# A ring of weight halves moved to six different distances (modulo 512 bytes) from the operands it is multiplied with

## The chip, the core and the metric

One NeuronCore of a Trainium2 chip runs the whole program. The metric is the device time of one execution in microseconds (us); the kernel before has a median of 2301.32 us over three runs. About 0.2% (4.6 us) is what a measurement of this kernel can tell from no change.

## The reference

One layer of a transformer-like trunk on a sequence of 512 tokens of width 2048, all in float32. With modulation vectors from a small matrix-vector product (`mod = silu(c) @ w_ada + b_ada`), it computes

```
h    = rms_norm(x) * (1 + sc1) + sh1
proj = h @ w_in                        # 2048 -> 7168 columns, seven groups of 1024
o_hg = gated linear recurrence (8 heads) on four of the groups
o_sb = stick-breaking attention (8 heads) on three of the groups
x    = x + g1 * (concat(o_hg, o_sb) @ w_out)      # 2048 -> 2048
h    = rms_norm(x) * (1 + sc2) + sh2
x    = x + g2 * ((silu(h @ w_gate) * (h @ w_up)) @ w_ffn_out)   # 2048 -> 2 x 5632 -> 2048
```

## The kernel before

**Three products for one.** Nearly all matrix products run in the format `float32r`. To keep float32's precision each operand is split in two halves: `hi`, the value rounded to `float32r`, and `lo`, the rest. One 128x128 block of a product is then three matmuls, `whi*xhi`, `whi*xlo` and `wlo*xhi`, added up in PSUM: in every group of three, two matmuls use a hi half of the weights and one a lo half. The halves of the weights are made on the fly by `split` (lines 212-222): ScalarE copies the raw tile into `hi` (line 220), VectorE subtracts `hi` from the raw tile into `lo` (line 221).

**The ring.** The halves live in the pool `wp`, in tiles of 4096 bytes per partition: tag `hi` with three buffers and tag `lo` with three buffers, six tiles in all, used in turn. The raw weights come into four tiles of 8192 bytes of the same pool. In the FFN, and after it, every fourth split goes to a spare pair instead (`spare[0]`, line 215): in the gate/up products that is a pair of tiles `hi2`, `lo2` in the pool `tp` (line 1106), whose matmuls the profile calls `ff_1hi`, `ff_1lo` and so on, where those of the ring are `ff_1h`, `ff_1l`; in the last product the pair lies inside an operand buffer (`spare_there`, line 1165).

**Where the tiles lie in a partition.** Pools are laid out one behind the other from the low end (constants, `wp`, the operands `hhi` and `hlo`, then `opA`, `opD` and others), and a few (`xop`, `tp`, `rp`, `zp`) from the high end downward. In `wp` the four raw tiles come first, then the three hi tiles at bytes 43808, 47904 and 52000, then the three lo tiles at 56096, 60192 and 64288. `hhi` starts at 68384, `hlo` at 101152, `opA` at 133920, `opD` at 166688. All these differ by multiples of 512 bytes. The spare pair `hi2`, `lo2` lies at 215008 and 219104: 146624 = 286 x 512 + 192 bytes above `hhi`, so its distance modulo 512 is 192. One column of a block is 4 bytes in each partition, a 128-column block of weights 512 bytes; every slice that a matmul of the ring takes starts a whole number of 512 bytes into its tile.

**Stages, in the order of the program**, and which operand of the matmul the ring's half is (a matmul loads its *stationary* operand of 128 columns with a weight load, and streams its *moving* operand past it):

- `st` (lines 286-332): hgrn2's values, 512 columns of ring half moving past slices of `hhi`/`hlo`.
- `sbp` (`sb_project`, line 337): attention's projections, 384 columns of ring half moving, with the attention itself (matmuls in plain float32) woven in.
- `hgf`, `hgq`, `hgg` (`mtile`, line 599): ring half stationary, 512 columns of `hhi`/`hlo` moving, with the recurrence woven in.
- `wo` (`wo_part`, line 808): ring half stationary, 512 columns moving; then its last tile and the first FFN columns (lines 917-980) with 256 columns moving.
- `ffA`, `ffB`, `ffC` (lines 1115-1157): the gate and up products in Strassen's form. For each of 42 column blocks there are seven products of 24 matmuls (8 blocks of the width times three), ring half or spare half stationary, 256 columns of `opA` to `opD` moving.
- `foA`, `foB`, `foC` (`multiply`, line 1183): the last product, also in Strassen's form, ring half moving with 512 columns.

The order of TensorE's work is written out by the program, with a small planner (`Clock`) that weaves in the attention and recurrence by estimated times. The tile framework adds the waits: a new tile of a ring position waits until the matmuls that read the old one are through.

Of the kernel before, what the change touches and what calls it, by code (L numbers as in the profile page):

```python
# [11 lines left out]
F32R = mybir.dt.float32r  # L12
# [5 lines left out]
P = 128  # L18
# [111 lines left out]
def trunk(ctx, tc, a):  # L130
# [6 lines left out]
    wp = ctx.enter_context(tc.tile_pool(name="wp", bufs=3))  # L137
# [6 lines left out]
    def acc(name):  # L144
        return psum.tile([P, T], F32, tag="acc", name=name)
# [22 lines left out]
    def small_col(base, i=0):  # L168
        return small[:, base + i:base + i + 1]
# [9 lines left out]
    def gemv(w, row, col):  # L179
        V.scalar_tensor_tensor(w, w, 1.0, row, op0=ALU.mult, op1=ALU.mult, accum_out=col)  # L180

    def finish_gain(comp, k0, k1):
        g, base = (gain1, C_N1) if comp == SC1 else (gain2, C_N2)
        V.scalar_tensor_tensor(g[:, k0:k1], mod[:, comp * KT + k0:comp * KT + k1], 1.0, small[:, base + k0:base + k1],
                               op0=ALU.add, op1=ALU.mult)

    def ada(comp, k):
        j = comp * KT + k
        c = slice(j, j + 1)
        gemv(row_load(a["w_ada"][j], f"ada{j}"), cond, mod[:, c])  # L190
        left[comp] -= 1
        if comp == SC1:
            V.tensor_add(mod[:, c], mod[:, c], small_col(C_BADA, j))
            finish_gain(comp, k, k + 1)
        elif not left[comp]:
            all_k = slice(comp * KT, comp * KT + KT)
            V.tensor_add(mod[:, all_k], mod[:, all_k], small[:, C_BADA + comp * KT:C_BADA + comp * KT + KT])
            if comp == SC2:
                finish_gain(comp, 0, KT)
# [7 lines left out]
        nc.sync.dma_start(r, src)  # L207
        return r

    spare, count = [], [0]  # L210

    def split(r, shape, name):
        count[0] += 1
        if spare and count[0] % 4 == 0:
            hi, lo = spare[0](shape, name)
        else:
            hi = wp.tile(shape, F32R, tag="hi", name=name + "h")
            lo = wp.tile(shape, F32R, tag="lo", name=name + "l")
        with tc.high_priority(offset=AHEAD):
            S.copy(hi, r)  # L220
            V.tensor_sub(lo, r, hi.bitcast(F32))  # L221
        return hi, lo

    def weights(src, shape, name):
        return split(load(src, shape, name), shape, name)
# [60 lines left out]
    for k in range(KT):  # L286
        xk = xo[:, k]
        if k == 0:
            for i in range(2):
                sl = slice(i * 1024, i * 1024 + 1024)  # L290
                gemv(r0[:, sl], cond[:, sl], lead[:, i:i + 1])
            j = SC1 * KT
            V.scalar_tensor_tensor(mod[:, j:j + 1], lead[:, 0:1], lead[:, 1:2], small_col(C_BADA, j), op0=ALU.add, op1=ALU.add)
            finish_gain(SC1, 0, 1)
            whi = wp.tile([P, 1024], F32R, tag="hi", name="wi0h")
            wlo = wp.tile([P, 1024], F32R, tag="lo", name="wi0l")
            for sl in (slice(0, T), slice(T, 2 * T)):
                S.copy(whi[:, sl], w0[:, sl])
                V.tensor_sub(wlo[:, sl], w0[:, sl], whi[:, sl].bitcast(F32))
        else:  # L300
            nc.sync.dma_start(xk, a["x"][:, k])
            ada(SC1, k)
            if k == 2:
                nc.sync.dma_start(cst, a["cst"])
            if k == KT - 1:
                nc.sync.dma_start(ident2, a["cst"][:, 0])
            whi, wlo = weights(a["w_hi"][k], [P, 1024], f"wi{k}")
        gk = gain1[:, k:k + 1]
        S.activation(hhi[:, k], xk, AF.Identity, scale=gk)
        V.scalar_tensor_tensor(hlo[:, k], xk, gk, hhi[:, k].bitcast(F32), op0=ALU.mult, op1=ALU.subtract)  # L310
        if k == 0:
            S.activation(ss1, xk, AF.Square)
        else:
            sq = sb.tile([P, T], F32, tag="qT" if k % 2 else "kT", name=f"sq{k}", bufs=1)
            S.activation(sq, xk, AF.Square)
            V.tensor_add(ss1, ss1, sq)
        for n in range(2):
            for t in range(4):
                ts_ = slice(t * P, t * P + P)
                cs = slice(n * T, n * T + T)  # L320
                out = banks[n * 4 + t]
                PE.matmul(out, hhi[:, k, ts_], whi[:, cs], start=(k == 0), stop=False)
                PE.matmul(out, hhi[:, k, ts_], wlo[:, cs], start=False, stop=False)
                PE.matmul(out, hlo[:, k, ts_], whi[:, cs], start=False, stop=(k == KT - 1))
# [12 lines left out]
    def sb_project(h):  # L337
        ps = [acc(f"sbp{h}_{t}") for t in range(4)]
        for c in range(8):
            if c % 2 == 0:  # L340
                raw = load(a["w_sb"][h, c // 2], [P, 2, 2, 384], f"wsb{h}_{c}")
            whi, wlo = split(raw[:, c % 2], [P, 2, 384], f"wsb{h}_{c}")
            pairs = [(kk, t) for kk in range(2) for t in range(4)]
            if c in (0, 7):
                pairs.sort(key=lambda p: p[1])
            for kk, t in pairs:
                k = 2 * c + kk
                ts_ = slice(t * P, t * P + P)
                out = ps[t][:, 0:384]
                PE.matmul(out, hhi[:, k, ts_], whi[:, kk], start=(k == 0), stop=False)  # L350
                PE.matmul(out, hhi[:, k, ts_], wlo[:, kk], start=False, stop=False)
                PE.matmul(out, hlo[:, k, ts_], whi[:, kk], start=False, stop=(k == KT - 1))
                clock.run()
        clock.until(lambda: h not in reuse or reuse[h] in done)
        if h in (0, 3):
            rows = scr[:, 0:3].rearrange("p a b -> p (a b)").rearrange("p (t c) -> p t c", t=4)
        else:
            rows = sb.tile([P, 4, 384], F32, tag="rows", name=f"rows{h}")
        for t in range(4):
            if t % 2:  # L360
                V.tensor_copy(rows[:, t], ps[t][:, 0:384])
            else:
                S.copy(rows[:, t], ps[t][:, 0:384])
        ready[h] = rows
# [234 lines left out]
    def mtile(src, name, xhi, xlo, out, nk=KT):  # L599
        n = 0  # L600
        raw = load(src, [P, nk, P], name)
        for c0 in range(0, nk, HALF):
            w = min(HALF, nk - c0)
            whi, wlo = split(raw[:, c0:c0 + w], [P, w, P], f"{name}_{c0}")
            for kk in range(w):
                three(out, whi[:, kk], wlo[:, kk], xhi[:, c0 + kk], xlo[:, c0 + kk], n == 0, n == nk - 1)
                n += 1
                clock.run()
# [314 lines left out]
    for i, hs in enumerate(halves):  # L923
        out = acc(f"wo{m}h{i}")[:, 0:HT]
        n = 0
# [304 lines left out]
    for u, (c, i) in enumerate(units):  # L1230
# [15 lines left out]
        for q, p in enumerate(ORDER):  # L1246
            out = {2: B[i], 7: C, 4: C}.get(p, A)
# [104 lines left out]
```

## Time and profile before

| | |
|---|---|
| three runs | 2303.38, 2301.32, 2300.13 us; median 2301.32 us |
| profiled execution, first to last instruction | 2299.2 us |
| TensorE (PE) busy | 2249.4 us, 98% of the span, 14171 matmuls |
| VectorE (DVE) busy | 1917.8 us, 83% |
| ScalarE (ACT) busy | 1160.6 us, 50% |
| DMA engines | 53% of the span, 190 GB/s on average |
| mean granted TensorE clock | 0.994 |

The profile gives the span of the profiled execution and not a device time of its own beside it; the span lies 2.1 us under the median of the runs. A row of a view of the profile names the line, the engine, the operation and the tiles (`out<-in,in`: for a matmul the moving operand first, then the stationary one), how many there were, the busy time and the mean duration of one in ns. Matmuls are pipelined, so the duration of one (about 280 ns) is longer than the time from the start of one to the start of the next, which is what a stream of matmuls costs; that pace is read from start times in the view in order of time.

### The profile page before, as it was taken

The numbers are of one execution on the slowest core, as the hardware profiler recorded it, in microseconds if no ns is written. First come the engines' busy times: TensorE is split into PE (matmuls) and PEld (weight loads), VectorE is DVE, ScalarE is ACT, GpSimd is POOL, SyncE is SP. The second block draws the span as 40 slices with busy tenths as digits, with TensorE's granted clock in tenths as the row PEclk, the third lists the DMA queues.
The fourth block names the chain that finished last, engine by engine and source line by source line (L and its number), as shares of the span: only waits on it lengthen the run. The fifth ranks groups of instructions, "written<-read, shape, count | busy, mean of one in ns | idle before, by whom it ended". The sixth has DMA issues, their size and how long they took to land.

```text
span 2299.2 us, 35729 instructions
## 1 busy us (share of the span) xinstructions
PE 2249.4 (98%) x14171; PEld 2050.2 (89%) x14171; DVE 1917.8 (83%) x2566; ACT 1160.6 (50%) x2015; POOL 10.7 (0%) x25
## 2 busy tenths in 40 slices
PE   7999899999999999999999999999999999999999
PEld 6899899888888788999999999999999977778787
DVE  8887779999888865699899988888888778888888
ACT  4316666565655522564454445454545544544453
POOL 0000000000000000000000000000000000000000
PEclk9999999999999999999999999999999999999999
DMA  9885546853322386346555645454443486665452
GB/s 368 319 317 218 174 145 227 304 183 111 128 93 74 130 303 214 105 151 225 189 204 185 220 143 175 143 174 143 150 160 129 166 314 232 238 220 213 154 200 76
DMA packets 114978, 437.69 MB, mean 190 GB/s; under 512 B 9822, under 2 KB 58236, under 8 KB 76796
## 3 DMA queue, kind: packets, MB, share of 16 engines
q1 hardware_dynamic: 114812, 435.42, 53.0%
q8 instruction: 111, 1.82, 0.3%
q14 instruction: 55, 0.45, 0.1%
HBM read 386.61 MB, written 48.77 MB: 189 GB/s over the span
## 4 chain that ended last, share of the span: by engine, by line
PE 77%; DVE 13%; DMA 3%; issue 3%; ACT 3%; SPq 0%; DVEq 0%; ACTq 0%
PE ffA L93 18%; PE foA L93 9%; PE ffC L93 9%; PE sbp L93 7%; PE wo L93 7%; PE foC L93 4%; PE ffB L93 4%; PE st L93 4%; PE hgf L93 4%; PE hgq L93 3%; PE hgg L93 3%; DMA opd<-fhi 1%; DVE ada L180 1%; DVE yraw L1190 1%; PE l L93 1%
## 5 line engine op out<-in xcount | busy, mean ns | idle before, releaser
L180 DVE SCALAR_TENSOR_TENSOR ada<-ada,cond 128x2048 f32<-128x2048 f32 x95 | 216.8, 2286 | 54.5 <-DMA ada<-in_w_ada 54.3
L93 PE MATMUL ffA<-opD,ff_3h 128*128 128x256 f32 x512 | 93.9, 284 | 1.8 <-ACT u L1018 1.7
L93 PE MATMUL ffA<-opB,ff_6h 128*128 128x256 f32 x512 | 94.1, 284 | 1.0 <-ACT ff_6h L220 1.0
L93 PE MATMUL ffB<-opA,ff_2h 128*128 128x256 f32 x512 | 93.5, 283 | 0.0
L93 PE MATMUL ffC<-opC,ff_4h 128*128 128x256 f32 x512 | 93.5, 283 | 0.0
L93 PE MATMUL ffA<-opC,ff_5h 128*128 128x256 f32 x496 | 90.7, 283 | 0.8 <-ACT b L1018 0.8
L93 PE MATMUL ffA<-opA,ff_1h 128*128 128x256 f32 x496 | 90.6, 283 | 0.0
L93 PE MATMUL ffC<-opB,ff_7h 128*128 128x256 f32 x496 | 90.6, 283 | 0.0
L221 DVE TENSOR_TENSOR wfo_0l<-wfo,wfo_0h 128x1024 fp32r<-128x1024 f32 x48 | 58.7, 1224 | 37.9 <-ACT wfo_0h L220 37.5
L93 PEld LDWEIGHTS ffA<-opD,ff_3h 128*128 128x128 f32 x512 | 79.7, 192 | 2.4 <-ACT u L1018 2.4
L93 PEld LDWEIGHTS ffA<-opB,ff_6h 128*128 128x128 f32 x512 | 80.1, 193 | 1.3 <-ACT ff_6h L220 1.2
L93 PEld LDWEIGHTS ffC<-opC,ff_4h 128*128 128x128 f32 x512 | 79.7, 192 | 0.0
L93 PEld LDWEIGHTS ffB<-opA,ff_2h 128*128 128x128 f32 x512 | 79.7, 192 | 0.0
L220 ACT CAST wfo_0h<-wfo 128x1024 fp32r<-128x1024 f32 x48 | 50.6, 1054 | 57.5 <-PE foA L93 50.4
L1092 ACT CAST fhi<-forms 128x512 fp32r<-128x512 f32 (+1 forms) x63 | 43.6, 692 | 68.5 <-DMA opd<-fhi 59.2
L93 PEld LDWEIGHTS ffA<-opC,ff_5h 128*128 128x128 f32 x496 | 77.2, 192 | 1.0 <-ACT b L1018 1.0
L93 PEld LDWEIGHTS ffC<-opB,ff_7h 128*128 128x128 f32 x496 | 77.3, 192 | 0.0
L93 PEld LDWEIGHTS ffA<-opA,ff_1h 128*128 128x128 f32 x496 | 77.2, 192 | 0.0
L93 PE MATMUL ffA<-opB,ff_6l 128*128 128x256 f32 x256 | 72.7, 284 | 0.0
L93 PE MATMUL ffC<-opC,ff_4l 128*128 128x256 f32 x256 | 72.4, 283 | 0.0
L93 PE MATMUL ffA<-opD,ff_3l 128*128 128x256 f32 x256 | 72.4, 283 | 0.0
L93 PE MATMUL ffB<-opA,ff_2l 128*128 128x256 f32 x256 | 72.4, 283 | 0.0
(1646 smaller groups left out, 7764.6 us busy)
## 6 DMA issues: line engine op xcount, KB each, us to landing
ada<-in_w_ada SPq DMA_DIRECT2D x95, 1024.0 KB, 5.2
wfo<-in_w_fo SPq DMA_DIRECT2D x16, 1024.0 KB, 5.9
yraw<-in_w_fo SPq DMA_DIRECT2D x16, 1024.0 KB, 4.8
fix<-in_w_fix SPq DMA_DIRECT2D x14, 1024.0 KB, 5.6
opd<-forms SPq DMA_DIRECT2D x44, 256.0 KB, 4.3
opd<-fhi SPq DMA_DIRECT2D x42, 256.0 KB, 4.3
opsC<-opd SPq DMA_DIRECT2D x10, 1024.0 KB, 5.1
opsA<-opd SPq DMA_DIRECT2D x9, 1024.0 KB, 7.2
```

What stands on the lines that cost most here:

```text
L93: self.engine.matmul(out, lhsT, rhs, **kw)
L180: V.scalar_tensor_tensor(w, w, 1.0, row, op0=ALU.mult, op1=ALU.mult, accum_out=col)
L220: S.copy(hi, r)
L221: V.tensor_sub(lo, r, hi.bitcast(F32))
L1092: S.copy(hi, R[:, q])
L1190: V.tensor_sub(*(t[:, k0:k0 + w] for t in (d, e, g)))
```

## The change

The tags `hi` and `lo` with three buffers each are replaced by six tags with one buffer each, used as three pairs in turn. Each tile is longer than its 4096 bytes of content by 64 to 384 bytes, and the content begins at an offset inside it. The spare pairs, the number and the order of all instructions on each engine's data, and all shapes stay.

```diff
+    pads = ((("h0", 64, 0), ("l0", 64, 0)), (("h1", 256, 0), ("l1", 128, 0)), (("h2", 192, 0), ("l2", 224, 32)))
+
+    def ring_pair(shape, name):
+        n = int(np.prod(shape[1:]))
+        out = []
+        for tag, before, after in pads[turns[0] % 3]:
+            t = wp.tile([P, 1024 + (before + after) // 4], F32R, tag=tag, name=name + tag[0], bufs=1)
+            t = t[:, before // 4:before // 4 + n]
...
+            out.append(t)
+        turns[0] += 1
+        return out
 
     def split(r, shape, name):
...
         else:
-            hi = wp.tile(shape, F32R, tag="hi", name=name + "h")
-            lo = wp.tile(shape, F32R, tag="lo", name=name + "l")
+            hi, lo = ring_pair(shape, name)
...
-            whi = wp.tile([P, 1024], F32R, tag="hi", name="wi0h")
-            wlo = wp.tile([P, 1024], F32R, tag="lo", name="wi0l")
+            whi, wlo = ring_pair([P, 1024], "wi0")
```

The six tiles take 4160, 4160, 4352, 4224, 4288 and 4352 bytes, 25536 together instead of 24576. Counted from the first, their contents begin at 64, 4224, 8576, 12800, 17088 and 21408. Everything laid out behind `wp` from the low end moves up by 960 bytes, `hhi` to 25536 behind the ring's start; what is laid out from the high end stays. Each content's start less `hhi`'s start, modulo 512, is then

| tile | h0 | l0 | h1 | l1 | h2 | l2 | spare pair of the FFN |
|---|---|---|---|---|---|---|---|
| distance before | 0 | 0 | 0 | 0 | 0 | 0 | 192 |
| distance after | 128 | 192 | 448 | 64 | 256 | 480 | 256 |

For example h0: 64 - 25536 = -25472, and -25472 + 50 x 512 = 128. The spare pair comes to 192 - 960 + 1024 = 256. `hlo` and `opA` to `opD` lie multiples of 512 behind `hhi`, so the row holds for them too. Where the ring's half is the moving operand, the distance of the stationary operand from it is the same number with its sign turned (128 becomes 384, 480 becomes 32).

More of the change, by code (lines that the diff above doesn't have):

```diff
@@ L208, in load @@
         return r
-    spare, count = [], [0]
+    spare, count, turns = [], [0], [0]
+    pads = ((("h0", 64, 0), ("l0", 64, 0)), (("h1", 256, 0), ("l1", 128, 0)), (("h2", 192, 0), ("l2", 224, 32)))
[5 more added lines that the diff above has]
+            t = t[:, before // 4:before // 4 + n]
+            if len(shape) == 3:
+                t = t.rearrange("p (a b) -> p a b", a=shape[1])
+            elif len(shape) == 4:
+                t = t.rearrange("p (a b c) -> p a b c", a=shape[1], b=shape[2])
+            out.append(t)
+        turns[0] += 1
+        return out
     def split(r, shape, name):
```

## The prediction

> **What bounds the kernel now.** I read first the page's busy times and the shares of the chain that ended last.
>
> ```profile
> PE 2249.4 (98%) x14171; PEld 2050.2 (89%) x14171; DVE 1917.8 (83%) x2566; ACT 1160.6 (50%) x2015; POOL 10.7 (0%) x25
> PE 77%; DVE 13%; DMA 3%; issue 3%; ACT 3%; SPq 0%; DVEq 0%; ACTq 0%
> ```
>
> TensorE is busy in 98% of the span, and 77% of the chain is its own work. A busy TensorE need not be at its best pace, so the pace is the question. Next, busy times by stage, in the order st, sbp (two rows), hgf to hgg, wo, first FFN columns, ffA to ffC, foA to foC; the pairs behind the length are PE, PEld, DVE, ACT (POOL too), then clock, DMA share and GB/s.
>
> ```profile
> 0.00:101.00 101.00, 89.22 (x386) 73.55 (x387) 84.50 (x127) 44.80 (x60) 1.68 (x9) 1.00 0.94 353
> 101.00:235.00 134.00, 130.49 (x733) 128.17 (x732) 108.59 (x134) 51.99 (x91) 0.00 (x0) 0.97 0.73 268
> 235.00:439.00 204.00, 196.67 (x1163) 184.98 (x1161) 166.21 (x240) 126.14 (x340) 0.00 (x0) 0.97 0.55 197
> 439.00:770.00 331.00, 328.22 (x1678) 275.76 (x1677) 289.25 (x541) 201.53 (x444) 9.05 (x16) 1.00 0.36 131
> 770.00:943.00 173.00, 170.28 (x764) 139.29 (x763) 107.96 (x133) 52.63 (x82) 0.00 (x0) 1.00 0.62 220
> 943.00:1004.00 61.00, 60.61 (x492) 59.51 (x490) 55.49 (x142) 51.80 (x120) 0.00 (x0) 1.00 0.30 100
> 1004.00:1849.00 845.00, 838.33 (x7052) 836.89 (x7052) 726.56 (x822) 419.79 (x612) 0.00 (x0) 1.00 0.50 175
> 1849.00:2299.20 450.20, 435.61 (x1917) 352.05 (x1916) 379.23 (x433) 211.91 (x269) 0.00 (x0) 0.99 0.56 201
> ```
>
> TensorE is full in every stage but the first, where the DMA engines are at 94%. The gate/up stage alone is 845 us. Of the other engines VectorE comes next everywhere, between 62% and 91%.
>
> **The pace, ring against spare pair.** In order of time, a stretch of products with the ring's halves (the first column is the start in us; rows that hold two matmuls end in x2):
>
> ```profile
> 1209.98 0.40 PE L93 MATMUL ffA<-opD,ff_3h 128*128 128x256 f32 x2
> 1210.22 0.28 PE L93 MATMUL ffA<-opD,ff_3l 128*128 128x256 f32 x1
> 1210.34 0.40 PE L93 MATMUL ffA<-opD,ff_3h 128*128 128x256 f32 x2
> 1210.58 0.28 PE L93 MATMUL ffA<-opD,ff_3l 128*128 128x256 f32 x1
> 1210.70 0.40 PE L93 MATMUL ffA<-opD,ff_3h 128*128 128x256 f32 x2
> ```
>
> and one with the spare pair's:
>
> ```profile
> 1031.17 0.39 PE L93 MATMUL ffA<-opA,ff_1hi 128*128 128x256 f32 x2
> 1031.40 0.28 PE L93 MATMUL ffA<-opA,ff_1lo 128*128 128x256 f32 x1
> 1031.51 0.39 PE L93 MATMUL ffA<-opA,ff_1hi 128*128 128x256 f32 x2
> 1031.74 0.28 PE L93 MATMUL ffA<-opA,ff_1lo 128*128 128x256 f32 x1
> 1031.85 0.39 PE L93 MATMUL ffA<-opA,ff_1hi 128*128 128x256 f32 x2
> ```
>
> Three matmuls take 0.36 us with the ring (120.0 ns each) and 0.34 us with the spare pair (113.3 ns): the same instruction, shape and moving operands, 6.7 ns less. That this is no accident of one stretch shows in the groups of the gate/up stage, whose last number before the second bar is the mean ns of one:
>
> ```profile
> L93 PE MATMUL ffA<-opA,ff_1h 128*128 128x256 f32 x495 | 90.5, 283 | 0.0
> L93 PE MATMUL ffA<-opA,ff_1hi 128*128 128x256 f32 x176 | 30.5, 276 | 0.0
> ```
>
> Again 7 ns apart. By the layout, the ring's weights lie 0 from the operand modulo 512, the spare pair's 192. Now the other widths, 384 columns in order of time, then 512 columns from the chain (start, length, what, count):
>
> ```profile
> 149.97 0.33 PE L93 MATMUL sbp<-wsb_2h,hhi 128*128 128x384 f32 x1
> ...
> 150.49 0.33 PE L93 MATMUL sbp<-wsb_2h,hhi 128*128 128x384 f32 x1
> ```
>
> ```profile
> 11.78 87.71 PE st L93 x378
> 812.72 130.55 PE wo L93 x574
> 2001.37 8.18 PE foA L93 x36
> ```
>
> Three matmuls of 384 columns take 0.52 us, 173.3 ns each; 130.55/574 is 227.4 ns and 8.18/36 is 227.2 ns for 512 columns. From 256 to 384 to 512 columns each step of 128 costs 53 to 54 ns, 0.42 ns a column, so 256 columns alone are 106.7 ns. The ring pays about 13.3 ns per matmul on top, whatever the width and whether its half is stationary (wo) or moving (sbp, foA); the spare pair pays 6.7. A charge per matmul and not per column fits the weight load, which is the same 128 columns each time and runs beside the matmul. My theory: the load and the moving stream disturb each other when their addresses agree modulo 512 bytes, and each such meeting costs 6.7 ns, the time of 16 columns or 64 bytes.
>
> The Trainium skill says the opposite: in "TensorE: Matmul & The Clock Gate", Part 2, on LDWEIGHTS, TensorE has two independent read ports into the state buffer, so that loading the next weights takes no read bandwidth from the running matmul. By that the six distances change nothing; the 7 ns between the two groups above speak against it, unless the spare pair is quicker for another reason.
>
> **The change part by part.**
>
> *Instructions and waits.* None is added or removed. The positions are still used in turn, three deep, so each split waits for the same earlier product as now; cost nothing. These waits sit on ScalarE and are covered by the other two pairs:
>
> ```profile
> ACT ff_2h L220 <- PE ffA L93: 39.1, 26, 1.9
> PE st L93 <- ACT hhi L309: 11.8, 1, 11.8
> PE foA L93 <- ACT O L1205: 3.6, 1, 3.6
> ```
>
> The copies wait up to 1.9 us for their slot, while TensorE itself waits long only at the start.
>
> *ScalarE and VectorE.* The copy and the subtraction now read and write at unlike distances. The spare pair does so already (raw 192 away):
>
> ```profile
> L220 ACT CAST ff_1hi<-wg3r 128x1024 fp32r<-128x1024 f32 x1 | 1.1, 1060 | 0.0
> L220 ACT CAST ff_1h<-wg4r 128x1024 fp32r<-128x1024 f32 x1 | 1.1, 1057 | 1.3 <-issue 1.3
> L221 DVE TENSOR_TENSOR ff_1lo<-wg19r,ff_1hi 128x1024 fp32r<-128x1024 f32 x1 | 1.2, 1227 | 0.3 <-ACT ff_1hi L220 0.3
> L221 DVE TENSOR_TENSOR ff_1l<-wg20r,ff_1h 128x1024 fp32r<-128x1024 f32 x1 | 1.2, 1227 | 1.6 <-ACT ff_1h L220 1.6
> ```
>
> 1060 against 1057 and 1227 against 1227 ns: cost nothing. They also price the waits above if their cover were gone: a product would then start later by at most one split, 1.06 + 1.23 us.
>
> *The ring's matmuls.* No row shows 64, 128, 256, 448 or 480; the ends are the rows at 0 (13.3 ns on top) and at 192 (6.7 ns). I take 192's price for h0, l0, h1, l1 and h2, which lie 64 bytes or more from 0, and 0's price for l2, which lies 32 bytes from it (480 = 512 - 32), inside the 64 bytes of one meeting. Of three matmuls one uses a lo half, and of three lo halves one is l2: 8/9 of the ring's matmuls save 6.7 ns, 5.9 ns on average. Where TensorE has slack or VectorE is close, part is lost:
> - Gate/up: 42 x 7 products of 24, less 73 that go to the spare pair, leaves 5304 matmuls, 31.4 us. At these paces 5304 x 120.0 + 1752 x 113.3 ns is 835 of the stage's 845 us, so TensorE is the limit; VectorE would rise from 726.56/845 (86%) to 89%. I keep 30.
> - First FFN columns (384, and 96 of wo's last tile): 480 x 5.9 = 2.8; VectorE 91%, ScalarE 85%: half, 1.5.
> - sbp (8 heads x 16 x 4 x 3): 1536 x 5.9 = 9.1, in a stage woven with attention's chains: two thirds, 6.
> - hgf to hgg (24 tiles x 16 x 3): 1152 x 5.9 = 6.8; VectorE 87%: two thirds, 4.5.
> - wo (15 x 16 x 3): 720 x 5.9 = 4.3; DMA 62%: 3.5.
> - foA to foC: 3/4 of 1848 (22 x 2 x 7 x 2 x 3) matmuls are the ring's, 1386 x 5.9 = 8.2; VectorE 84%: two thirds, 5.5. Its spare pair lies inside an operand buffer and stays at 0.
> - st (16 x 8 x 3): 384 x 5.9 = 2.3 us; the DMA engines at 94% would be late next: nothing.
>
> *The spare pair of the gate/up stage* moves from 192 to 256. It could gain or lose up to 6.7 ns in each of 1752 matmuls, 11.7 us either way. I take nothing: 256 is nearer to 192 than to 0.
>
> Sum: 30 + 1.5 + 6 + 4.5 + 3.5 + 5.5 = 51 us. The profiled span of 2299.2 becomes 2248; the median of the runs, 2.1 us above it, becomes **2250 us**, 2.2% less.
>
> The same page of the Trainium skill, Part 1 ("Wait — 56ns, not 53.3ns?"), gives a warm matmul N/2.4 GHz plus about 2.5 ns, so an estimate by it is 109.2 ns for 256 columns; no row here shows a float32r matmul that fast.
>
> **The rivals.** If all six tiles paid 192's price, the sum would be 51 x 9/8 = 57 us (2244 us), the measure for what follows.
> 1. *Only tiles nearer to 192 than to 0 gain* (h0, l0, h2: 16 + 8 + 16 of every 72 matmuls, 5/9). For it: nothing is known between the rows. Against: the price comes in steps of 64 bytes. 57 x 5/9 = 32 us, 2269 us.
> 2. *The distance counts modulo 128 or 256.* Then 256 is as bad as 0 for h2 and the spare pair (modulo 128 also h0). Gain 5/9 of 57, less 11.7: 20 us, 2281 us; modulo 256 only h2 is lost among the hi halves (6/9 with l2 lost): 38 less 11.7, 2275 us. Against it only that I know of one good distance.
> 3. *Some distances are better than 192.* If half of the 6.7 ns that are left goes as well, the ring gains 57 x 1.5 = 86 and the spare pair 1752 x 3.3 = 5.8 us: 2209 us. For it: 6.7 ns still stand above the columns.
> 4. *The distance does nothing*, and the spare pair is quick for where it lies (the high end) or for its single buffer: 2301 us. For it: pace and place change together in the only two cases known. The rule of the Trainium skill quoted above is of this kind.
> 5. *Slower: 192 is the rare good distance.* The ring stays at 120 ns, since all multiples of 64 but that one meet, and the spare pair, moved to 256, falls to 120 too: 1752 x 6.7 = +11.7 us, 2313 us. It decides where the ring's gain is under a fifth of 57 us. For it: the only good distance known is the one that the spare pair gives up.
>
> **How the numbers follow.** Chances: forecast 0.47 (2250, own range 2236 to 2264), rival 1 0.16, rival 2 0.10, rival 3 0.12, rival 4 0.08, rival 5 0.07. Faster by over 0.2% (4.6 us, what a measurement can tell) are the forecast and rivals 1 to 3: 0.85; within 0.2% rival 4: 0.08; slower rival 5: 0.07. The range runs from rival 3 to just past rival 2, 2209 to 2284 us; left out are rivals 4 and 5 and the tail below, under 0.2.
>
> **What would show it.** Right: gate/up matmuls of h0, h1, h2, l0, l1 start 113 ns apart, l2's 120; the seven products' groups at 276 ns; 512 columns at 220 ns in wo and foA; the gate/up stage near 815 us; splits still 1.06 and 1.23 us. A ring still at 120 ns throughout makes the theory wrong (rivals 4, 5, told apart by the spare pair's pace); gate/up at 113 with the span unmoved would mean VectorE has taken over.

## The result, and the profile after

The changed kernel takes 2324.93 us (median of 4 runs, 2324.32 to 2329.3) against 2301.15 us for the kernel before on the same chip: a ratio of 1.0105, 95% interval 1.0091 to 1.0118, so about 24 us slower. The forecast was 2250 us, the range 2209 to 2284, the chance of slower 0.07. The profiled execution has a span of 2323.0 us, 23.8 us more than before.

Busy times and the shares of the chain that ended last, from the page of the changed kernel:

```profile
PE 2270.0 (98%) x14171; PEld 2050.7 (88%) x14171; DVE 1919.3 (83%) x2566; ACT 1159.8 (50%) x2015; POOL 10.7 (0%) x25
PE 49%; DVE 10%; DMA 3%; issue 2%; ACT 1%; SPq 0%; DVEq 0%; ACTq 0%
```

TensorE does the same 14171 matmuls and is busy 20.6 us longer; VectorE and ScalarE are as busy as before, within 2 us. Busy times by stage of the changed kernel, cut at the same places of the program as the table in the prediction:

```profile
0.00:104.00 104.00, 92.46 (x388) 74.82 (x389) 85.00 (x127) 45.21 (x60) 1.68 (x9) 1.00 0.92 343
104.00:239.00 135.00, 131.23 (x746) 128.43 (x745) 110.64 (x137) 53.73 (x95) 0.00 (x0) 1.00 0.74 274
239.00:440.00 201.00, 194.31 (x1150) 182.83 (x1149) 164.85 (x238) 124.44 (x337) 0.00 (x0) 0.98 0.55 195
440.00:773.00 333.00, 331.06 (x1674) 275.38 (x1672) 289.42 (x542) 201.56 (x445) 9.05 (x16) 1.00 0.36 130
773.00:957.00 184.00, 176.40 (x762) 142.16 (x762) 108.60 (x131) 52.52 (x81) 0.00 (x0) 0.97 0.58 207
957.00:1018.00 61.00, 60.12 (x493) 58.83 (x491) 55.40 (x142) 51.83 (x120) 0.00 (x0) 1.00 0.28 100
1018.00:1864.00 846.00, 838.97 (x7055) 837.36 (x7056) 726.42 (x823) 419.07 (x612) 0.00 (x0) 1.00 0.50 175
1864.00:2323.00 459.00, 445.45 (x1913) 350.85 (x1912) 378.99 (x433) 211.44 (x269) 0.00 (x0) 0.99 0.55 197
```

Against before: st 104 for 101, sbp 336 for 338, hgf to hgg 333 for 331, wo 184 for 173, first FFN columns 61 for 61, gate/up 846 for 845, foA to foC 459 for 450.2. The gate/up stage, from which 30 of the forecast's 51 us were to come, is where it was. The loss lies in wo (+11) and in the last product (+9).

The pace in the gate/up stage of the changed kernel, in order of time, a spare product (one of the seven products of a column block, with the spare pair's halves) and the ring product behind it:

```profile
1208.91 0.40 PE L93 MATMUL ffA<-opA,ff_1hi 128*128 128x256 f32 x2
...
1209.63 0.39 PE L93 MATMUL ffB<-opA,ff_2h 128*128 128x256 f32 x2
...
1212.43 0.28 PE L93 MATMUL ffA<-opB,ff_6h 128*128 128x256 f32 x1
```

From 1208.91 to 1209.63 lie six matmuls of the spare pair, 120.0 ns each where they took 113.3; from 1209.63 to 1212.43 the 24 of a ring product, 116.7 ns each where they took 120.0. The groups say it for the whole stage (mean ns of one before the second bar; before: 283 and 276):

```profile
L93 PE MATMUL ffA<-opA,ff_1h 128*128 128x256 f32 x496 | 88.9, 280 | 0.0
L93 PE MATMUL ffA<-opA,ff_1hi 128*128 128x256 f32 x176 | 32.1, 283 | 0.0
```

And 512 columns, from the chain of the changed kernel (start, length, what, count):

```profile
2058.47 8.35 PE foA L93 x36
```

8.35/36 is 231.9 ns; before it was 8.18/36 = 227.2. So the ring gained a little at 256 columns, the spare pair lost all it had, and wide matmuls became slower.

A second difference is not a pace. The order of TensorE's work is not the same: by the names in the traces, which leave out buffer numbers, 346 of its 14171 places hold another matmul than before, 85 of them together in wo and 261 in foA to foC (the expectation of e13 below counts 394). The text above says that the change leaves the order as it is and that the kernel before uses its ring positions in turn; neither holds, as the last two experiments show.

### The profile page after: what moved, and what is told of

It reads as the page before. It is cut to its first block, busy times and chain, and to the rows that moved or that the text cites. A ratio compares the mean times of both kernels' runs of the same rounds, so it can differ in the third digit from the quotient of the medians.

```text
span 2323.0 us, 35722 instructions
## 1 busy us (share of the span) xinstructions
PE 2270.0 (98%) x14171; PEld 2050.7 (88%) x14171; DVE 1919.3 (83%) x2566; ACT 1159.8 (50%) x2015; POOL 10.7 (0%) x25
## 4 chain that ended last, share of the span: by engine, by line
PE 49%; DVE 10%; DMA 3%; issue 2%; ACT 1%; SPq 0%; DVEq 0%; ACTq 0%
PE ffA L93 16%; PE foA L93 9%; PE ffC L93 8%; PE wo L93 6%; PE ffB L93 4%; PE foC L93 4%; DVE yraw L1203 1%; DMA ada<-in_w_ada 1%; DMA opd<-fhi 1%; DVE wfo L1267 1%; DVE T L1203 1%; DVE wfo_0l L235 1%; PE foB L93 1%; DVE wfo L1203 1%; DVE x L902 0%
## 5 line engine op out<-in xcount | busy, mean ns | idle before, releaser
L235 DVE TENSOR_TENSOR wfo_0l<-wfo,wfo_0h 128x1024 fp32r<-128x1024 f32 x48 | 58.7, 1223 | 46.8 <-ACT wfo_0h L234 46.8
L234 ACT CAST wfo_0h<-wfo 128x1024 fp32r<-128x1024 f32 x48 | 50.3, 1049 | 90.0 <-PE foA L93 61.5
L93 PE MATMUL ffA<-opA,ff_1h 128*128 128x256 f32 x496 | 88.9, 280 | 0.0
```

Source lines behind the costliest of these rows:

```text
L93: self.engine.matmul(out, lhsT, rhs, **kw)
```

## The experiments

Theory A is the prediction's: meetings cost 6.7 ns each and are fewest at most distances other than 0 modulo 512. Against it stood at first its rivals 2 (the distance counts modulo 256) and 5 (192 is the rare good distance). When neither was enough, a third was formed. Theory F: the pace is a beat that weight loads and streams fall into, which depends on the distance modulo 256, on the columns and on what ran just before. Theory O came last: part of the loss is the order of the work and has nothing to do with distances.

Pace below always means from the start of one matmul to the start of the next, meaned over a stage with the interruptions left out (at 256 columns, starts 135 ns or more apart), worked out from all start times of the trace in that stage (of which the fences show a few). The ring's pace in the gate/up stage takes in the first FFN columns. Ratios are to the kernel before on the same chip, with 95% intervals.

**One distance for the whole ring: e1, e2, e3.** One tile is put between ring and operands; tags, buffers and order are those of before.

```diff
+    hp.tile([P, 80], F32, name="gap0")      # e1; P, 240 in e2; P, 64 in e3
     hhi = hp.tile([P, KT, T], F32R, tag="hhi", name="hhi")
```

e1, ring at 192: 

> The kernel before with 320 bytes left free between the ring and hhi, so that all six tiles lie 192 from the operands (spare pair 384). Theory A (the distance of each pair decides, 192 is good): gate/up ring matmuls 113.3 ns apart, 512 columns 220 ns, time about 2244 us. Theory B (what counts is that all distances of a stream are equal, so that load and stream fall into a steady beat; unequal ones break it): a steady pace at every width, no scatter, total 2244 to 2301 us. Theory C (the place of an operand itself counts, not the distance): operands at 96 modulo 512 instead of 288, anything from 2240 to 2325 us, and the same in the ring and the spare pair.

e2, ring at 64: 

> The kernel before with 960 bytes left free between the ring and hhi: the shift of the change alone, operands where the change has them, all six ring tiles at distance 64, spare pair at 256. Theory A: the ring has one price, whatever 64 costs, and the spare pair 120 ns as in the changed kernel. Theory B: no scatter, 512 columns back at 227 ns or 220 ns, total at most 2312 us (2301 and the spare pair's 11.7). Theory C: 512 columns at 231 ns as in the changed kernel's last product, total about 2320 us.

e3, ring at 256: 

> The kernel before with 256 bytes left free between the ring and hhi: ring at 256 everywhere, spare pair at 448. Theory A: ring gate/up matmuls 120 ns apart as the changed kernel's spare pair at 256. Theory B: steady at 113.3 or 120 ns, 512 columns at 220 or 227 ns. Theory C: operands at 32 modulo 512, not to be told beforehand, scatter as in the changed kernel (512 columns 230 to 234 ns).

Measured: e1 2311.74 us, 1.0038 (1.0024 to 1.0053); e2 2311.27 us, 1.0040 (1.0025 to 1.0055); e3 2301.31 us, 0.9994 (0.9985 to 1.0004). Ring and spare pair in e3, from its groups:

```profile
L93 PE MATMUL ffA<-opA,ff_1h 128*128 128x256 f32 x496 | 90.6, 283 | 0.0
L93 PE MATMUL ffA<-opA,ff_1hi 128*128 128x256 f32 x176 | 30.5, 276 | 0.0
```

They are the rows of before to the ns: 256 is as good as 0 for the ring, and for the spare pair (192 moved to 448) as good as 192. The distance counts modulo 256 bytes. Now 512 columns in the last product, from the chains of e1 and of e2:

```profile
2008.81 8.41 PE foA L93 x36
```

```profile
2009.88 8.27 PE foA L93 x36
```

233.6 and 229.7 ns against 227.2 at distance 0: at the very distance that was thought good, wide matmuls are slower than at the one thought bad. In the gate/up stage the ring runs at 117.8 ns in e1 and 117.4 in e2, not at 113.3. Theory A falls here: its price at 192 is true of the spare pair in the kernel before, but not of the ring.

The stages of e1 and e2 show one thing more. Counted from the moving to the stationary operand, the ring at 192 is at 192 where its half is stationary and at 64 where it moves, and the ring at 64 the other way round. At 192, 512 columns take 229.8 and 229.0 ns (e1, hgf to hgg and wo) and 228.9 (e2, st); at 64 they take 233.3 (e1, st) and 233.4 (e2, hgf to hgg and wo). So it is this difference that counts, whichever of the two is the ring's half, and the period is not 128, by which 64 and 192 would be alike.

**The spare pair alone: e4.** Everything from the raw tiles to the operands moves together, so the ring keeps distance 0, and the spare pair, which hangs from the high end, comes to 256.

```diff
     ident2 = const.tile([P, P], F32, name="ident2")
+    const.tile([P, 112], F32, name="gap1")
```

> The kernel before with 448 bytes left free behind the constants, so that raw tiles, ring and operands all move together: ring and operands at 224 modulo 512 (the place of the changed kernel's operands), distance 0, spare pair at 256. Theories A and B: ring 120 ns, 512 columns 227 ns as before, spare pair 120 ns, so 2301 + 11.7 = 2313 us. Theory C: the last product at 231 ns per 512 columns, as the changed kernel shows at distance 0; total 2320 us or more.

Measured: 2311.84 us, 1.0042 (1.0027 to 1.0057). The spare pair's group in e4:

```profile
L93 PE MATMUL ffA<-opA,ff_1hi 128*128 128x256 f32 x176 | 32.2, 283 | 0.0
```

It is at the ring's 283 ns, and the first FFN columns and the gate/up products together last 904.8 us, from their first matmul to the last product's, against 893.5 before: +11.3, where rival 5 had priced 1752 x 6.7 = 11.7. The ring's pace is unmoved, so moving both operands by 448 bytes does nothing as long as their distance stays.

**The ring at the spare pair's very places: e5.** Is it the pair of places modulo 256, and not their difference, that made the spare pair quick? Here ring and operands lie modulo 256 where the spare pair and its operands lie in the kernel before.

```diff
     ident2 = const.tile([P, P], F32, name="ident2")
+    const.tile([P, 48], F32, name="gap1")
...
+    hp.tile([P, 16], F32, name="gap0")
     hhi = hp.tile([P, KT, T], F32R, tag="hhi", name="hhi")
```

> 192 bytes free ahead of the raw tiles and ring, 64 behind it: ring at 224 modulo 256, operands at 32 modulo 256, exactly the pair of places that the spare pair had in the kernel before. The spare pair keeps these places too (distance 448). Theory D (the places modulo 256 of both operands count, in the ring as in the spare pair): gate/up ring matmuls at 113.3 ns, 35 us less in that stage; the 512-column stages not known, from 220 to 234 ns; total 2260 to 2290 us. Theory E (113.3 ns belongs to the spare pair as a tile, by its single buffer or its place at the high end): ring at 117 to 120 ns, total 2300 to 2312 us.

Measured: 2307.91 us, 1.0033 (1.0019 to 1.0046), 117.6 ns for ring and spare pair alike, 233.3 and 232.5 ns in st and foA. The places do not explain it either. But the trace of e5 has two stretches, of six and of seven products, that run otherwise. Beginning and end of the second, in order of time:

```profile
1210.66 0.40 PE L93 MATMUL ffC<-opB,ff_7h 128*128 128x256 f32 x2
...
1211.02 0.40 PE L93 MATMUL ffC<-opB,ff_7h 128*128 128x256 f32 x2
...
1211.99 0.39 PE L93 MATMUL ffA<-opC,ff_5hi 128*128 128x256 f32 x2
...
1212.67 0.39 PE L93 MATMUL ffA<-opC,ff_5hi 128*128 128x256 f32 x2
...
1230.02 0.39 PE L93 MATMUL ffC<-opB,ff_7h 128*128 128x256 f32 x2
...
1230.36 0.39 PE L93 MATMUL ffC<-opB,ff_7h 128*128 128x256 f32 x2
...
1231.23 0.40 PE L93 MATMUL ffA<-opC,ff_5h 128*128 128x256 f32 x2
...
1232.29 0.40 PE L93 MATMUL ffA<-opC,ff_5h 128*128 128x256 f32 x2
```

Three matmuls take 0.36 us in the first pair of rows (117.7 ns by all of that product), then six take 0.68 (113.3), and so do all products up to the pair at 1230, where three take 0.34. After it nine take 1.06 (117.8). Both changes of pace fall on a short interruption, and all these products have the same distance, 448. The first stretch, from 1113.4 us, begins with an interruption too. One distance thus has two paces, and it keeps the one it has until something interrupts it. That is theory F.

**Alignment: e6, e7, e8.** All three move operands to whole multiples of 64 bytes, which they are not in the kernel before: e6 everything at distance 0, e7 ring at 448, e8 operands alone.

```diff
+    const.tile([P, 8], F32, name="gap1")                 # e6, e7
...
+    hp.tile([P, 16], F32, name="gap0")                   # e7; P, 8 in e8
...
+            tp.tile([P, 8], F32, name="gap2", bufs=1)    # e7, at f == 2
```

e6: 

> Everything from the raw tiles on moved by 32 bytes: raw, ring and operands begin on a multiple of 64 bytes, distance 0; the spare pair does not (distance 160). Theory D, with pieces of 64 bytes (a block that begins in the middle of a piece touches one piece more): one step of 6.7 ns less per matmul, 113.3 ns at 256 columns, 220 ns at 512, total about 2230 us. If only differences modulo 256 count: ring 120 ns, 512 columns 227 ns, spare pair not known, 2295 to 2312 us.

e7: 

> As the run with 32 bytes ahead, and 64 more behind the ring, and the tiles of the gate/up stage's high end moved down by 32: everything on multiples of 64 bytes, ring at distance 192 modulo 256, spare pair at 64. Theory D: 106.7 to 113.3 ns at 256 columns, under 227 ns at 512, total 2200 to 2240 us. Theory E or differences alone: 117 to 120 ns, 229 to 234 ns, total 2300 to 2315 us.

e8: 

> The kernel before with 32 bytes free behind the ring: operands on a multiple of 64 bytes, raw tiles and ring 32 short of one (distance 480, spare pair 160). Theory D with pieces of 64 bytes: 113.3 ns or less in gate/up where the operand moves, 227 ns or more in st, sbp and the last product where the ring moves; total 2255 to 2290 us. Otherwise scatter as in the changed kernel, 117 to 118 ns and 230 to 234 ns, total 2305 to 2325 us.

Measured: e6 2310.56 us, 1.0041 (1.0026 to 1.0056), ring 119.9 and spare pair 119.6 ns, 226.8 ns in st; e7 2306.21 us, 1.0015 (1.0005 to 1.0026); e8 2315.3 us, 1.0051 (1.0035 to 1.0068). No pace of e7 and e8 is known. e6 is e4 again with the spare pair at 160: alignment does nothing at distance 0, and 160 is no better for the spare pair than 256. For the rest the three times only say that none of these places is a gain; whether alignment changes a pace at 448 or 480 stays open.

**Does a product at distance 0 set the quick beat? e9, e10, e11, e12.** In the kernel before, the spare pair at 192 always runs behind ring products at 0. In e9 the two change places: the operands of the gate/up products lie 64 bytes further on in their tiles, so that the ring is at 192 there while all wide stages stay at 0, and the spare pair is moved to 0. e10 is e9 with the spare pair at 192 too, so that nothing at distance 0 is left in the stage. e11 is e10 with the first of the eight operand blocks of four of the seven products put at 0. e12 is the changed kernel with its spare pair put back to 192.

```diff
-    early = fh.tile([P, 2, HALF, 2, HT], F32R, tag="b1", name="opA")
+    early = at(fh, "b1", "opA", 8192 + 16, 16, "p (a j h t) -> p a j h t", shape=(2, HALF, 2, HT), a=2, j=HALF, h=2)
...
-    late = hp.tile([P, 2, HALF, 2, HT], F32R, tag="hhi", name="opB")
+    late = in_hhi("opB", 16, (2, HALF, 2, HT), "p (a j h t) -> p a j h t", a=2, j=HALF, h=2)
...
+            tp.tile([P, 32], F32, name="gap2", bufs=1)    # e9; P, 48 in e10 and e11; P, 16 in e12
```

e9: 

> The kernel before with the gate/up operands (opA to opD) 64 bytes further on inside their tiles, while the operands of all other stages stay at distance 0; ring in gate/up at 192 modulo 256, spare pair moved by 128 bytes to distance 0. Theory F (the pace depends on the state that the stream is in: matmuls at distance 0 bring it at once into a fixed beat of 120.0 ns, and a product at 192 that follows keeps 113.3 ns until something interrupts it): ring at 113.3 ns, spare pair at 120 ns, 5304 x 6.7 - 1752 x 6.7 = 24 us less in the stage, total about 2278 us. Theory A (the distance alone, at 117.7 ns for 192 as in the run with all at 192): ring 117.7, spare pair 120 ns, total about 2300 us.

e10: 

> As the run before, but the spare pair too lies at 192: no product of the gate/up stage is at distance 0. Theory F: nothing sets the beat again after an interruption; most products at 117.7 ns, some stretches at 113.3; 7056 x 117.7 ns is 830 us, 5 us under the kernel before, total 2292 to 2300 us. If 192 alone made 113.3 ns once the other stages stay at 0: 7056 x 113.3 = 799 us, 36 us less, total 2266 us.

e11: 

> Ring and spare pair at 192 as in the run without distance-0 products, but the first of the eight operand blocks of four of the seven products lies at distance 0: three matmuls at the start of each of these products. Theory F, if three matmuls are enough to set the beat: 12 of 168 matmuls at 120, the rest at 113.3 ns, 803 instead of 835 us for the stage, total about 2270 us. If they are not enough: 117.7 ns, total 2295 to 2300 us.

e12: 

> The changed kernel with the spare pair of gate/up moved by 64 bytes, back to the distance of 192 that it had before. Theory A: spare pair back at 113.3 ns, 11 us less, total about 2313 us. Theory F: no product at distance 0 precedes it, so it does not come back to 113.3 but runs at 116 to 119 ns; total 2317 to 2325 us.

Measured: e9 2299.12 us, 0.9983 (0.9975 to 0.9992); e10 2298.09 us, 0.9988 (0.9977 to 0.9998); e11 2300.97 us, 1.0003 (0.9994 to 1.0012); e12 2327.2 us, 1.0111 (1.0098 to 1.0125). In e9, in order of time, a ring product, a spare product at 0, a stall and the next ring product:

```profile
1223.70 0.39 PE L93 MATMUL ffA<-opC,ff_5h 128*128 128x256 f32 x2
...
1224.38 0.39 PE L93 MATMUL ffA<-opC,ff_5h 128*128 128x256 f32 x2
...
1224.72 0.40 PE L93 MATMUL ffC<-opC,ff_4hi 128*128 128x256 f32 x2
...
1227.24 0.40 PE L93 MATMUL ffC<-opC,ff_4hi 128*128 128x256 f32 x2
...
1228.56 0.50 PE L93 MATMUL ffA<-opD,ff_3h 128*128 128x256 f32 x2 [0.80 <-ACT u L1028]
...
1229.02 0.40 PE L93 MATMUL ffA<-opD,ff_3h 128*128 128x256 f32 x2
...
1229.72 0.40 PE L93 MATMUL ffA<-opD,ff_3h 128*128 128x256 f32 x2
```

The ring runs at 113.3 ns (six in 0.68), the product at 0 at 120.0 (21 in 2.52), and behind the stall of 0.80 us the ring, at the same distance as ever, at 116.7 (six in 0.70) and 117.7 over that product. Behind the next spare product it is back at 113.3. Over the stage the ring has 114.6 ns in e9, 117.5 in e10, 118.2 in e11; the spare pair at 192 has 117.8 in e10 and 117.7 in e12, where in the kernel before it has 113.5. So a whole product at distance 0 ahead sets the quick beat at 192 in most cases: of the 153 ring products of e9 that no interruption parts from the spare product ahead, 141 run at 113.3 ns. An interruption among the ring's products ends it: none of the 33 that come behind one has it. Three matmuls at 0 (e11) do not set it. A product at 0 is not the only way into it, though: the stretches of e5 have nothing at 0 around them, and in e2, with the ring at 64, the first FFN columns run at 114.0 ns. What sets the beat there stays open.

e12 shows the same for the changed kernel: with 192 given back, its spare pair still does not get its old pace. No whole product at distance 0 stands ahead of it any more; of the changed ring only h2 (256) is at 0 modulo 256. The ring of e12 shows most plainly what the product ahead does. Here is the stretch that was shown for the changed kernel, with the spare pair now at 192:

```profile
1207.80 0.40 PE L93 MATMUL ffA<-opA,ff_1hi 128*128 128x256 f32 x2
...
1210.62 0.41 PE L93 MATMUL ffB<-opA,ff_2h 128*128 128x256 f32 x2
...
1213.51 0.40 PE L93 MATMUL ffA<-opB,ff_6h 128*128 128x256 f32 x2
```

The ring product behind the spare product takes 120.4 ns a matmul (24 in 2.89 us), where the changed kernel has 116.7. It has the same instructions and distances in both; only the pair that the product ahead of it uses lies 64 bytes elsewhere. Over the stage the ring products directly behind the spare pair have 116.8 ns in the changed kernel and 119.9 in e12, while the second and third behind it have 118.8 and 117.6 in both. By the move the spare pair gained 1752 x 2.2 = 3.9 us, and the ring lost 1768 x 3.1 = 5.5.

The time of e12 also carries theory O's term, which was not known when it was expected and which e12 shares with the change.

By these paces e9 should have gained (5304 + 384) x 5.4 - 1752 x 6.4 = 19.5 us from the first FFN columns to the last product, and gained 2.2 (891.3 for 893.5). The waits of TensorE in it:

```profile
PE ffA L93 <- ACT u L1028: 4.5, 4, 1.9
PE ffA L93 <- ACT b L1028: 3.3, 5, 1.3
PE ffC L93 <- ACT c L1028: 3.2, 9, 0.6
```

In the kernel before the same view has 1.7 for u and 0.8 for b: TensorE now runs ahead of the copies that take its products out of PSUM. All its waits in the gate/up products come to 15.9 us against 6.6. All interruptions, also the short ones that this view does not list, stand 29 us above 118 ns a matmul in e9 and 12 us before: that is the 17 us that are missing. e9 and e10 are the fastest versions here, by less than the 0.2% that a measurement can tell from no change.

**The order of the work: e13 and e14.** The paces leave some 6 us open, and matmuls stand elsewhere in the order. The cause is in the tags. Three buffers under one tag give each new tile whichever position is free when its split is placed. One buffer under each of six tags gives it the position that its turn in the program names, free or not. e13 makes this part of the change alone: six tags without padding, so that all distances are those of before and the order is the changed kernel's.

```diff
-    pads = ((("h0", 64, 0), ("l0", 64, 0)), (("h1", 256, 0), ("l1", 128, 0)), (("h2", 192, 0), ("l2", 224, 32)))
+    pads = ((("h0", 0, 0), ("l0", 0, 0)), (("h1", 0, 0), ("l1", 0, 0)), (("h2", 0, 0), ("l2", 0, 0)))
```

e14 makes the other part: tags `hi` and `lo` with three buffers as before, and TensorE's order is that of before. In the gate/up stage it has the changed kernel's distances modulo 256, paired otherwise.

```diff
+    wherein = ((64, 32), (32, 32), (64, 96))
...
+        for tag, place in zip("hl", wherein[turns[0] % 3]):
+            t = wp.tile([P, 1064], F32R, tag={"h": "hi", "l": "lo"}[tag], name=name + tag)
+            t = t[:, place // 4:place // 4 + n]
```

e13: 

> Leaves every distance of the kernel before (ring at 0, spare pair at 192) and takes from the change only the six tags used in a fixed turn; with them 394 of TensorE's matmuls stand at other places of its order, in the stages wo and foA to foC, as in the changed kernel. If distances are the whole of the change: the time of the kernel before, 2301 us, within 2 us, and wo as long as before. If the order costs what the paces leave open (some 5 to 7 us, most of it in wo): 2306 to 2309 us, with the paces of before (226.7 ns at 512 columns, 120.0 for the ring and 113.3 for the spare pair in the gate/up stage), PE busy near 164 of the 173 us of wo and not 170.

e14: 

> The other half: tags hi and lo with three buffers each as before, so that TensorE's order is that of the kernel before to the last matmul, but with slots of 4256 bytes and contents at an offset in them, so that the distances modulo 256 in the gate/up stage are the change's (0, 128 and 192 for the three hi halves, 64, 192 and 224 for the lo halves, spare pair 256) and unlike 0 in most of the others. If distances are the whole of the change: 2325 us as the changed kernel. If the order costs 5 to 7 us of it: 2317 to 2320 us, the paces near those of the changed kernel (229 to 236 ns at 512 columns, 117 to 118 for the ring, 120 for the spare pair), and wo without the three waits for ohi, olo and orowhg at its start.

Measured: e13 2312.97 us, 1.0054 (1.0041 to 1.0066); e14 2313.76 us, 1.0053 (1.0039 to 1.0067), beside 2300.66 us. Each half is worth 12 to 13 us, and the two ratios multiplied are 1.0107: the whole of the change's 1.0105. The order costs twice what was expected of it. That its paces are those of before shows in e13's chain (8.17/36 = 226.9 ns):

```profile
2010.98 8.17 PE foA L93 x36
```

Where it loses shows in one stretch of wo. The same window of the kernel before, and then of e13 (length, PE, PEld, DVE, ACT, POOL, clock, DMA, GB/s):

```profile
796.00:811.00 15.00, 14.09 (x69) 10.84 (x68) 10.74 (x16) 3.50 (x14) 0.00 (x0) 1.00 0.76 275
```

```profile
796.00:811.00 15.00, 9.12 (x32) 6.33 (x31) 12.31 (x17) 4.61 (x14) 0.00 (x0) 0.66 0.82 297
```

32 matmuls instead of 69, at a granted clock of 0.66. In e13's order of time:

```profile
796.86 0.39 PE L93 MATMUL hgo<-vh,dgs 128*128 128x128 f32 x2
800.70 1.09 PE L98 MATMUL hgo<-cst,orowhg 128*128 128x128 f32 x4 [3.45 <-DVE orowhg L387]
803.28 1.22 PE L93 MATMUL wo<-ohi,wo_0h 128*128 128x512 f32 x2 [1.50 <-ACT ohi L813]
805.44 0.80 PE L93 MATMUL wo<-olo,wo_0h 128*128 128x512 f32 x1 [0.94 <-DVE olo L814]
...
808.39 0.63 PE L93 MATMUL wo<-ohi,wo_8h 128*128 128x512 f32 x1
808.81 0.63 PE L93 MATMUL wo<-olo,wo_8h 128*128 128x512 f32 x1
```

This is the end of the recurrence's last head: its output is normalised and split before TensorE can finish wo's tiles 0 and 1, whose halves `wo_0h` stay in use until then. ScalarE's splits of tiles 2 and 3 (raw tiles `wo2r` and `wo3r`), first in the kernel before and then in e13:

```profile
788.20 1.05 ACT L220 CAST wo_8h<-wo2r 128x1024 fp32r<-128x1024 f32 x1 [0.34 <-PE wo L93]
803.20 1.04 ACT L220 CAST wo_8h<-wo3r 128x1024 fp32r<-128x1024 f32 x1 [3.35 <-PE wo L93]
```

```profile
787.49 1.05 ACT L234 CAST wo_8h<-wo3r 128x1024 fp32r<-128x1024 f32 x1 [0.33 <-PE wo L93]
806.27 1.05 ACT L234 CAST wo_8h<-wo2r 128x1024 fp32r<-128x1024 f32 x1 [3.04 <-PE wo L93]
```

In the kernel before, tile 2 and then tile 3 fill that time with the heads already done: by the order of the program their splits take the one position that tiles 0 and 1 do not hold, one after the other. With a fixed turn the split of tile 2 gets the position that tile 0 holds. So it has to wait for the very work that it was to cover, and only tile 3 is left as cover. TensorE stands 3.45, 1.50 and 0.94 us, and the granted clock falls: 0.42 us from start to start at 808.39, where 0.227 is normal. By "TensorE: Matmul & The Clock Gate", Part 1, of the Trainium skill, a window of about 3.4 us without work halves TensorE's clock until it has been busy again; the row with 3.45 us idle and those behind it agree. wo grows by 7.9 us in e13 (194.2 for 186.3, from its first matmul to the next stage's), foA to foC by 6.4 (451.9 for 445.5, to the last matmul's start). The latter comes in some nine steps of 0.3 to 1.1 us, which were not followed to single waits.

For e14 the spare pair's group and a row of the chain:

```profile
L93 PE MATMUL ffA<-opA,ff_1hi 128*128 128x256 f32 x176 | 32.1, 283 | 0.0
```

```profile
2011.37 8.41 PE foA L93 x36
```

They are within 2 ns of the changed kernel's paces, and wo grows by 3.7 us only.

## Why the prediction was wrong, by its own steps

Stage lengths of the kernel before, from the first matmul of a stage to that of the next (in the last row to the last matmul), in us, and what the steps and the profiled executions add to them. The 96 matmuls of wo's last tile count with wo, so 0.3 of the 1.5 us for the first FFN columns stands there:

| stage | before | forecast | after | e13, order alone | e14, distances alone |
|---|---|---|---|---|---|
| st | 88.9 | 0 | +2.8 | -0.1 | +3.2 |
| sbp | 338.5 | -6 | -2.5 | -0.4 | -2.9 |
| hgf to hgg | 330.5 | -4.5 | +2.5 | -0.1 | +3.4 |
| wo with its last tile | 186.3 | -3.8 | +11.4 | +7.9 | +3.7 |
| first FFN columns and gate/up | 893.5 | -31.2 | +0.5 | +0.5 | +0.4 |
| foA to foC | 445.5 | -5.5 | +9.3 | +6.4 | +4.5 |
| sum | | -51 | +24.0 | +14.2 | +12.3 |

These are single executions, and differences of 2 to 3 us in a row can be chance. In e3, which has the paces and the order of the kernel before, wo is 2.5 us longer: 12 of its first matmuls stand 0.42 us apart (granted clock 0.77 from 765 to 780 us, where the kernel before has 1.00 at that place). The changed kernel has 8 such matmuls there and e14 has 7, some 1.5 us each; e13 has none there.

- **The price of a distance: the step that failed first.** "I take 192's price for h0, l0, h1, l1 and h2" carried a price from one case (256 columns, spare pair at 192, behind products at 0) to six other distances, to other widths and to another neighbourhood. e1 shows that it does not even hold for the ring at 192. At 256 columns the ring's term measures 5304 x 2.2 = 11.7 us (117.8 for 120.0 ns), not 30. Even a larger one need not have shortened the stage: in e9 paces worth 19.5 us gave 2.2, for TensorE came to wait, which the step "TensorE is the limit" did not allow for.
- **"Whatever the width."** A charge of 13.3 ns does stand on every width at distance 0, but at 512 columns it is the least that was met: stages at one other distance ran at 228.9 to 233.4 ns (e1, e2). The terms of the stages with 384 and 512 columns, 6 + 4.5 + 3.5 + 5.5 = 19.5 us of gain in the forecast, came to a loss: their rows for e14 in the table, with st's, add up to +11.9 us.
- **The spare pair, taken at nothing.** Its price "either way" was 11.7 us, and it came at its bad end: 119.9 ns for 113.5 in 1752 matmuls, 11.2 us. The reason for nothing, that 256 is nearer to 192 than to 0, fails on the period: modulo 256 it is 0. The loss cancels the ring's gain, which is why the gate/up stage stands still. Rival 5 had the price of this half, and rival 2 the period; neither saw that wide matmuls lose. That rival 5's 2313 us is the time of e14, the distances alone, is luck: its ring was to stay at 120 ns, and in e14 the ring gains about what the wide stages lose. (Rival 2's sum for modulo 128 counts l2 as gaining, where the one for modulo 256 has it lost; with l2 lost it is 4/9, 14 us and 2287 us.)
- **"The positions are still used in turn, three deep ... cost nothing."** This step failed by 12.3 us (e13's median against the kernel before on its chip; 14.2 in the profiled execution), as much as all distances together. The waits that the prediction listed for ScalarE were the right place to look; it did not ask what a fixed turn does where halves are held long, as `wo_0h` is.
- **Right:** the splits cost the same (1049 ns for ScalarE's copies and 1223 for VectorE's subtractions in wfo's group of 48, where VectorE's had 1224 before), and TensorE, busy in 98% of the span, stayed the limit in the changed kernel.
- The Trainium skill's rule that was weighed in the prediction, that a weight load takes no read bandwidth from the running matmul, does not carry the conclusion that distances change nothing: e4 changes no distance of the gate/up stage but that of the spare pair, and the stage grows by 11.3 us. Whether load and stream meet in reading or elsewhere, no run shows.

Shown are the paces, their period, their dependence on what ran before, and the cost of the order: e13 and e14 together make up the whole loss. What inside TensorE makes such a beat is not shown, and the paces of single distances in the changed kernel's mix were not tried one by one.

## What to carry to other kernels

A pace that is read from one group of instructions holds for its width and for what runs around it; before it is multiplied by thousands of other instructions, one run with the whole ring at that one distance (e1) would have shown that it does not carry over. Tags with one buffer each are not the same as one tag with three: where some tiles are held long, a fixed turn makes the work that was to cover a wait wait for it. If a change of layout goes together with a change in how buffers are handed out, run each of them alone.

## What the runs showed of the hardware that was not expected

- The time from one float32r matmul to the next, each with its own weight load, depends on the distance of the two operands modulo 256 bytes. At 0 it is steady: 120.0, 173.3 and 226.7 ns for 256, 384 and 512 columns. At other distances 256 columns take 113.3 to 120 ns and 512 columns mostly 229 to 236 (229 at 192 from the moving to the stationary operand, 233 at 64).
- At 192 and 256 columns there are two paces, 113.3 and 117.7 ns, with the same instructions and distances. The quicker was met behind a whole product at distance 0 (e9, and the spare pair before) and twice after an interruption (e5), and was lost at an interruption.
- Three matmuls together mostly stand above their columns by whole multiples of 6.67 ns, the time of 16 columns: at 256 columns 3, 4, 5 or 6 of them (340, 346.7, 353.3 and 360 ns over 320), at 512 columns 6 in the steady case.
- The same matmuls at the same distances had 116.8 ns behind a product at distance 0 and 119.9 ns behind one at 192 (the changed kernel and e12): a pace belongs to a sequence of matmuls, not to one of them.
